# One list sets the order of a hybrid decoder layer: the first half's last projections and the second half's tokens move ahead of pooling and scores

## The chip, the cores and the metric

The kernel runs on one core of a Trainium2 chip. The metric is the device time of one execution in microseconds (us), the median of repeated runs. A profile is one further execution, recorded by the hardware; its span goes from the first instruction to the last.

## What is computed

One layer for 1024 prompt tokens and 8 decode tokens, 1024 channels wide:

```python
p = rmsnorm(x) @ w_in             # 512 pooling + 1792 RWKV columns
u, q = p[..., :512], p[..., 512:]
# A: four groups of 128, trailing windows 2, 4, 8, 16
d = (cs[end] - cs[end - win]) / cnt - u
pool = (d @ pool_w[g]) * pool_scale
# B: RWKV-7, 8 heads of 64
qs = q + (shift(q) - q) * shift_mu
r, k, v, zw, za, zg = split(qs)   # 512, 512, 512, 64, 64, 128
decay = exp(-exp(-softplus(-(w0 + tanh(zw) @ w_lora_up)) - 0.5))
S = S * decay + (S @ aa) * bb + v * k    # token by token
y = S @ r                                # then norm, bonus, gate
x = x + concat(pool, y) @ w_out
x = x + relu(rmsnorm(x) @ w_up)**2 @ w_down
```

## The kernel before

Channels lie on partitions, tokens along the free side. The prompt is cut into four **token blocks** (0 to 255, 256 to 511, 512 to 767, and 768 to 1023 with the 8 decode tokens); blocks 0 and 1 are the first **half**, blocks 2 and 3 the second. Every large fp32 product is made of three passes of a shorter type (`gemm`, L183): tokens are split into `xh` and `xl` and weights into `wh` and `wl`, and each of the eight k-tiles gives three matmuls. So one 128-column tile of the input projection takes 24 matmuls per token block; its result is a tile `pj<m>_<b>` (m the column tile, b the block). Column tiles 0 to 3 are the pooling groups, 4 to 15 the r, k and v of four head pairs, 16 and 17 the low-rank inputs.

The recurrence is done in chunks of 64 tokens. The kernel is written as functions, and one list, `ORDER`, says in which order they are recorded; a scheduler then fixes each engine's queue, with priority by the list, and `tc.high_priority(offset=...)` pulls what stands under it ahead. The letters of the list, with their tiles:

- R0 to R7 (`rkv`): projections of k, r and v of a *unit*, which is a head pair in one half (0 to 3 first half, 4 to 7 second).
- S0 to S7 (`stage1`): the unit's decay and scores. TensorE makes `pw`, `pa`, `pk`, `pb`, `sc` and the transposes `bkt`, `vt`; between them stand chains on VectorE and ScalarE.
- I0 to I7 (`inverse`): the inverse of a triangular matrix, for two units in one token block. It doubles on VectorE, goes once out to memory and back (`inv`, `TX`) and ends in the matmuls `pi`. Its buffers exist once, so one inverse follows another.
- C0 to C7 (`lead_chain`): the state's walk over four chunks (`pcs`, `py`, L588 to L622), always pulled ahead by priority.
- P00, P01, P02 and P10, P11, P12 (`pools`): pooling, first and second half, in three parts. Part 0 has the projections and window sums of groups 0 and 1; part 1 the projections and sums of groups 2 and 3, and the products `po` of groups 0 and 1; part 2 the products `po` of groups 2 and 3. The weight `pw_sb` has one buffer.
- T (`later_tokens`): token blocks 2 and 3. They use the two buffers of `xh` and `xl`, so block 2 can be written only when block 0's last projection has been read, and block 3 after block 1's. The raw tokens lie in the four `wr` buffers that raw weights use too.
- L (`low_rank(1)`): column tiles 16 and 17 of the second half. Q and D are small (rows for the pooling state; the start of the decode tokens).

SyncE's queue issues token loads and the inverse's transfers; GpSimd's issues weights, `pw_sb` and the stores of the mixers' results (`mix`). After the list come the out projection `mx` of the first half, which overlaps C6, I7, C7 and the decode tokens, then that of the second half and the MLP (`up`, `dn`).

Of the kernel before, what the change touches and what calls it, by code (L numbers as in the profile page):

```python
# [16 lines left out]
D = 1024  # L17
NP = 1024
NDEC = 8
T = NP + NDEC  # L20
BLK = [(0, 512), (512, 260), (772, 260)]
SEG = [(0, 256), (256, 256), (512, 256), (768, 264)]
HALF = [(0, 512), (512, 520)]
# [4 lines left out]
LEADX = 300  # L28
# [8 lines left out]
NWH = 6  # L37
NX = 2
QUEUE = 1
ORDER = """R0 S0 R1 S1 P00 I0 Q P01 C0 I1 P02 C1 R2 S2 R3 T S3 L I2 R4 C2 I3 R5 C3 S4 S5 I4 R6 C4 I5 R7 C5 S6 S7 I6 P10 C6 I7 P11 P12 D"""  # L40
NBV = 4
NSEG = 4

# [49 lines left out]
def _build(ctx, nc, tc, I, O, dbg):  # L93
    V, A, PE, SY, GP = nc.vector, nc.scalar, nc.tensor, nc.sync, nc.gpsimd

    def f32(ap):
        return ap.bitcast(F32)
# [49 lines left out]
    def sigm(out, in_, bias, scale, last_bias=0.0):  # L147

        act(out, in_, AF.Exp, bias=bias, scale=scale)
        V.tensor_scalar(out, out, BIG, None, ALU.min)  # L150
        act(out, out, AF.Ln, bias=1.0)
        act(out, out, AF.Exp, scale=-1.0, bias=last_bias)


    def weights(src, into=None):

        out = []
        n = int(np.prod(src.shape[1:]))
        for o in range(0, n, 512):
            w = min(512, n - o)  # L160
            raw = wp.tile([P, 512], F32, tag="wr", name="wr", bufs=NWR)
            if len(src.shape) > 2:
                GP.dma_start(raw.rearrange("p (m c) -> p m c", c=P), src)
            else:
                GP.dma_start(raw[:, :w], src[:, o:o + w])
            if into:
                h, l = into
            else:
                h = wp.tile([P, 512], F32R, tag="wh", name="wh", bufs=NWH)
                l = wp.tile([P, 512], F32R, tag="wl", name="wl", bufs=NWH)  # L170
            with tc.high_priority(offset=LEADW):
                act(h[:, :w], raw[:, :w])
                V.tensor_tensor(l[:, :w], raw[:, :w], f32(h[:, :w]), op=ALU.subtract)  # L173
            out += [(h[:, c:c + P], l[:, c:c + P]) for c in range(0, w, P)]
        return out
# [26 lines left out]
    def token_block(b):  # L202

        c0, n = SEG[b]
        xh = xp.tile([P, KT, 266], F32R, tag="xh", name=f"xh{b}", bufs=NX)
        xl = xp.tile([P, KT, 266], F32R, tag="xl", name=f"xl{b}", bufs=NX)
        rs = xp.tile([P, 266], F32, tag="rs", name=f"rs{b}", bufs=NX)
        X[b] = (xh, xl, rs)
        if b:
            for t, q in zip(X[b][:2], X[b - 1]):  # L210
                act(t[:, :, 0:2], f32(q[:, :, 256:258]))
        acc = big(f"acc{b}", "f" if b % 2 else "e")[:, :512].rearrange("p (k t) -> p k t", k=2)
        raw = []

        def parts(k):
            if b == 0:
                xr = big(f"xr{b}_{k}", ("u0", "u1", "d0", "d1")[k // 2])
            elif b == 1:
                xr = s1.tile([P, 512 if k > 2 else 520], F32, tag=("w", "a", "t", "kk")[k // 2], name=f"xr{b}_{k}")
            else:  # L220
                xr = wp.tile([P, 512], F32, tag="wr", name=f"xr{b}_{k}", bufs=NWR)
            xr = xr[:, :512].rearrange("p (k t) -> p k t", k=2)
            raw.append(xr)
            SY.dma_start(xr, I["xT"][:, k:k + 2, c0:c0 + 256])
            for i in range(2):
                x, g, h = xr[:, i, :], col(V_G1, k + i), xh[:, k + i, 2:258]
                act(h, x, scale=g)
                V.scalar_tensor_tensor(xl[:, k + i, 2:258], x, g, f32(h), ALU.mult, ALU.subtract)

        def square(k):  # L230
            xr = raw[k // 2]
            if k:
                act(xr, xr, AF.Square)
                V.tensor_tensor(acc, acc, xr, op=ALU.add)
            else:
                act(acc, xr, AF.Square)

        for k in range(0, KT, 2):
            parts(k)
            if b > 1:  # L240
                square(k)
            if b == 0 and k == 2:
                yield
        yield
        if b < 2:
            for k in range(0, KT, 2):
                square(k)
        ss = (ps_i if b < 2 else ps_d).tile([P, 512], F32, tag="i" if b < 2 else "d", name=f"ss{b}")
        for i in range(2):
            PE.matmul(ss[:, :256], ON, acc[:, i, :], start=i == 0, stop=i == 1)  # L250
        if b == 3:
            xd, xg = (s1.tile([P, KT, NDEC], F32, tag=x, name=f"xd{x}") for x in ("t", "kk"))
            SY.dma_start(xd, I["xT"][:, :, NP:])
            V.tensor_tensor(xg, xd, vec[:, V_G1:V_G1 + 8].unsqueeze(2).to_broadcast([P, KT, NDEC]), op=ALU.mult)
            act(xh[:, :, 258:266], xg)
            V.tensor_tensor(xl[:, :, 258:266], xg, f32(xh[:, :, 258:266]), op=ALU.subtract)
            V.tensor_tensor(xg, xd, xd, op=ALU.mult)
            V.tensor_reduce(xd[:, 0, :], xg.rearrange("p k b -> p b k"), axis=AX.X, op=ALU.add)
            PE.matmul(ss[:, 256:264], ON, xd[:, 0, :], start=True, stop=True)
        ms, t = (s1.tile([P, 264], F32, tag="pr", name=f"{x}{b}", bufs=3) for x in ("ms", "tt"))  # L260
        with tc.high_priority(offset=LEADX if b > 1 else 0):
            rstd(rs[:, 2:n + 2], ss[:, :n], ms[:, :n], t[:, :n])
            if b:
                act(rs[:, 0:2], X[b - 1][2][:, 256:258])
        yield
# [9 lines left out]

    ahead, late = {}, {}

    def project(m, half, use):
        w = ahead.pop(m, None) or weights(I["w_in"][m])
        for b in (2 * half, 2 * half + 1):  # L280
            if b in late:
                with tc.high_priority(offset=LEADX):
                    next(late.pop(b))
            project_block(m, w, b, use, 0 if b else 2)
# [29 lines left out]
    def low_rank(half):  # L314
        n = HALF[half][1]
        z0 = big(f"z0{half}", "f")
        zw, za = (zp.tile([P, 520], F32R, tag=x, name=f"{x}{half}") for x in ("zw", "za"))
        z1 = zp.tile([P, 520], F32, tag="z1", name=f"z1{half}", bufs=2)
        shifted(12, half, z0)
        shifted(13, half, z1)  # L320
        sigm(z0[0:64, :n], z0[0:64, :n], 0.0, 2.0)
        V.tensor_scalar(z0[0:64, :n], z0[0:64, :n], -2.0, 1.0, ALU.mult, ALU.add)
        for z, r, q in ((zw, R[0], R[1]), (za, R[1], R[0])):
            act(z[r, :n], z0[r, :n])
            V.tensor_tensor(z[q, :n], z0[r, :n], f32(z[r, :n]), op=ALU.subtract)
        sigm(z1[:, :n], z1[:, :n], 0.0, -1.0)
        Zt[half] = (zw, za, z1)
# [491 lines left out]
    def later_tokens():  # L819
        with tc.high_priority(offset=LEADX):  # L820
            late.update((b, token_block(b)) for b in (2, 3))
            next(late[2])
            ahead[16] = weights(I["w_in"][16])
            next(late[3])

    st_d = ExitStack()
    dec = []
# [20 lines left out]
    x1 = []  # L848

    def open_x1(half):  # L850
        c0, n = HALF[half]
        xq = open_pool(ctx, f"x1{half}", side="right", reuse_waits="tile")
        x1.append(xq.tile([P, KT, n], F32, name=f"x1{half}"))
        for k in range(0, KT, 4):
            SY.dma_start(x1[half][:, k:k + 4, :], I["xT"][:, k:k + 4, c0:c0 + n])


    def x1s(m, c, n):

# [23 lines left out]
    open_x1(0)  # L883
    with tc.tile_pool(name="opa", bufs=1, side="right", reuse_waits="tile") as op:
        ops = [mixed(op, k, 0, NMA) for k in range(KT)]
        for m in range(KT):
            out_block(m, weights(I["w_out"][m]), ops, 0, 0, 512)
            next(dec, None)
# [46 lines left out]
    ps_u = open_pool(ctx, "psu", 4, space=PSUM)  # L935
    with tc.tile_pool(name="opb", bufs=1, reuse_waits="tile") as op:
        ops = [mixed(op, k, 1, 3) for k in range(KT - 1)]
        for m in range(KT):
            w = weights(I["w_out"][m, :, :(KT - 1) * P])
            for o in (0, 260):  # L940
                out_block(m, w, ops, 1, o, 260)
        norm2(0, 512, lambda x: op.tile([P, 512], F32, tag="n2", name=x, bufs=2))
        last = [mixed(op, KT - 1, 1, 3)]
        w7 = [w for m in (0, 4) for w in weights(I["w_out"][m:m + 4, :, (KT - 1) * P:].rearrange("m p c -> p m c"))]
        for m in range(KT):
            for o in (0, 260):
                out_block(m, w7[m:m + 1], last, 1, o, 260)
# [4 lines left out]
    w = weights(I["w_up"][0])  # L952
# [20 lines left out]
    for g in range(7):  # L973
        ups_of(4 * g + 4)
        for m in range(KT):
            w = weights(I["w_down"][g, m])
# [7 lines left out]
    ws = [weights(I["w_down"][7, m], None if m < 4 else [x[:, m, :] for x in w7]) for m in range(KT)]  # L984
# [103 lines left out]
```

## Time and profile before

| | before |
|---|---|
| median of 3 runs | 1372.07 us (1369.88 to 1374.78) |
| the profiled execution | 1369.46 us |
| its span | 1367.7 us |
| TensorE busy | 1304.4 us (95%) |
| VectorE busy | 806.9 us (59%) |
| ScalarE busy | 555.2 us (41%) |
| GpSimd busy | 152.2 us (11%) |
| TensorE's mean granted clock | 0.976 |

Busy shares are means over the whole span: the first third holds the input projection and the recurrence, where several engines work, the rest the MLP, where TensorE does. The granted clock is a share of 2.4 GHz. Names such as `L774` are lines of the kernel file of before; in the changed file the lines behind the new function stand 17 lower (L791).

### The profile page before, as it was taken

Reading aid. Unit: us, or ns where it says so; the run is one execution under the profiler, and the core shown is the slowest. Engines: PE = TensorE matmul, PEld = TensorE weight load, DVE = VectorE, ACT = ScalarE, POOL = GpSimd, SP = SyncE. Lnnn points to the kernel's source line nnn. Section 1 sums busy time; section 2 is a strip of 40 time slices with the busy share of each in tenths; the row PEclk is TensorE's granted clock in tenths of the full one; section 3 lists DMA queues with packets and bytes.
Section 4 is the critical chain, followed back from the end, with each engine's and each line's share of the span. In section 5 each row is a group of like instructions: output and inputs, shape, how many; then the busy total and the mean of one; then the engine's idle time right before and its main releaser. Section 6 shows DMA issues by size and latency. Waiting matters only on the chain.

```text
span 1367.7 us, 24214 instructions
## 1 busy us (share of the span) xinstructions
PE 1304.4 (95%) x9748; PEld 1149.8 (84%) x9748; DVE 806.9 (59%) x1782; ACT 555.2 (41%) x1261; POOL 152.2 (11%) x301
## 2 busy tenths in 40 slices
PE   6999996999999899999999999999999999999996
PEld 6988775878877676798999999999999999999986
DVE  7887577747866765748644535445444354453447
ACT  7655766766767667626211212112111121121123
POOL 3112001111100110120010100100000100000000
PEclk9999996999999899999999999999999999999998
DMA  7234123221321542431111111111111111111103
GB/s 226 70 80 115 44 61 74 77 52 54 71 50 42 160 127 79 158 132 60 47 55 39 55 47 40 54 40 47 54 39 55 47 43 50 45 48 48 47 7 124
DMA packets 81647, 94.52 MB, mean 69 GB/s; under 512 B 52504, under 2 KB 58776, under 8 KB 81528
## 3 DMA queue, kind: packets, MB, share of 16 engines
q0 software_dynamic: 20480, 66.04, 15.1%
q1 hardware_dynamic: 59728, 25.10, 7.3%
q8 instruction: 76, 1.25, 0.4%
q10 hardware_dynamic: 1328, 1.85, 0.4%
q14 instruction: 35, 0.29, 0.1%
HBM read 79.67 MB, written 13.51 MB: 68 GB/s over the span
## 4 chain that ended last, share of the span: by engine, by line
PE 77%; ACT 7%; DVE 6%; issue 5%; DMA 3%; POOL 1%; SPq 0%; DVEq 0%; POOLq 0%; ACTq 0%
PE dn L183 26%; PE up L183 26%; PE pj L183 7%; PE mx L183 5%; PE sc L415 2%; PE pcs L599 1%; PE pcs L593 1%; ACT SV L100 1%; DMA cst<-in_consts 1%; ACT TT L100 1%; PE py L589 1%; DVE tm L517 1%; ACT ys L100 1%; PE pcs L588 1%; DVE wl L173 1%
## 5 line engine op out<-in xcount | busy, mean ns | idle before, releaser
L100 ACT ACTIVATE wh<-wr 128x512 fp32r<-128x512 f32 x230 | 143.2, 626 | 357.8 <-PE dn L183 276.2
L183 PE MATMUL up<-h2h,wl 128*128 128x260 f32 (+1 forms) x768 | 245.6, 320 | 0.0
L183 PE MATMUL up<-h2h,wh 128*128 128x260 f32 (+1 forms) x768 | 245.1, 320 | 0.5 <-DVE u L930 0.5
L183 PE MATMUL up<-h2l,wh 128*128 128x260 f32 (+1 forms) x768 | 244.9, 320 | 0.0
L183 PE MATMUL dn<-uh,wl 128*128 128x512 f32 (+1 forms) x720 | 231.0, 321 | 0.0
L183 PE MATMUL dn<-ul,wh 128*128 128x512 f32 (+1 forms) x720 | 230.6, 320 | 0.0
L183 PE MATMUL dn<-uh,wh 128*128 128x512 f32 (+1 forms) x720 | 230.3, 320 | 0.0
L969 DVE TENSOR_TENSOR x<-dn,x 128x260 f32<-128x260 f32 (+1 forms) x192 | 99.1, 516 | 189.6 <-PE dn L183 189.6
L183 PE MATMUL pj<-xh,wh 128*128 128x258 f32 (+3 forms) x576 | 174.8, 303 | 10.8 <-ACT wh L100 9.7
L173 DVE TENSOR_TENSOR wl<-wr,wh 128x512 fp32r<-128x512 f32 x230 | 156.4, 684 | 41.0 <-ACT wh L100 37.6
L183 PE MATMUL pj<-xh,wl 128*128 128x258 f32 (+3 forms) x576 | 172.0, 299 | 0.0
L183 PE MATMUL pj<-xl,wh 128*128 128x258 f32 (+3 forms) x576 | 171.6, 298 | 0.0
L183 PEld LDWEIGHTS up<-h2l,wh 128*128 128x128 f32 x768 | 144.5, 188 | 12.3 <-DVE h2l L912 0.6
L183 PEld LDWEIGHTS up<-h2h,wh 128*128 128x128 f32 x768 | 144.2, 188 | 11.7 <-DVE u L930 0.9
L183 PEld LDWEIGHTS up<-h2h,wl 128*128 128x128 f32 x768 | 144.4, 188 | 11.1
L183 PEld LDWEIGHTS dn<-ul,wh 128*128 128x128 f32 x720 | 135.5, 188 | 10.9 <-issue 0.2
L183 PEld LDWEIGHTS dn<-uh,wh 128*128 128x128 f32 x720 | 135.7, 188 | 10.5
L183 PEld LDWEIGHTS dn<-uh,wl 128*128 128x128 f32 x720 | 135.4, 188 | 10.6 <-issue 0.2
L100 ACT ACTIVATE uh<-u 128x260 fp32r<-128x260 f32 (+1 forms) x96 | 47.2, 492 | 238.6 <-DVE u L931 238.6
L183 PEld LDWEIGHTS pj<-xh,wh 128*128 128x128 f32 x576 | 112.4, 195 | 16.5 <-ACT wh L100 9.7
L930 DVE SCALAR_TENSOR_TENSOR u<-up,rs 128x260 f32<-128x260 f32 (+1 forms) x96 | 49.5, 517 | 120.8 <-PE up L183 114.3
L183 PEld LDWEIGHTS pj<-xl,wh 128*128 128x128 f32 x576 | 112.6, 195 | 3.9 <-issue 2.6
(291 smaller groups left out, 2088.5 us busy)
## 6 DMA issues: line engine op xcount, KB each, us to landing
wr<-in_w_in POOLq DMA_DIRECT2D x72, 256.0 KB, 3.1
wr<-in_w_up POOLq DMA_DIRECT2D x64, 256.0 KB, 2.9
wr<-in_w_down POOLq DMA_DIRECT2D x64, 256.0 KB, 2.9
wr<-in_w_out POOLq DMA_DIRECT2D x26, 256.0 KB, 3.3
xr<-in_xT SPq DMA_DIRECT2D x16, 256.0 KB, 3.7
mr<-mix SPq DMA_DIRECT2D x8, 260.0 KB, 3.5
x<-in_xT SPq DMA_DIRECT2D x2, 1040.0 KB, 7.9
blk<-AA SPq DMA_DIRECT2D x16, 128.0 KB, 2.6
```

The lines of the kernel that those rows point to most:

```text
L100: A.activation(out, in_, func, bias=bias, scale=scale, **k)
L173: V.tensor_tensor(l[:, :w], raw[:, :w], f32(h[:, :w]), op=ALU.subtract)
L183: PE.matmul(ps, lhs, rhs, start=i == 0, stop=i == n - 1)
L415: PE.matmul(scs[h][:, c, :], BK[R[h], c, :, :], AR[R[h], c, :, h, :], start=True, stop=True)
L517: V.tensor_tensor(pr[:, q], l[:, q].unsqueeze(2).to_broadcast([64, m, m, m]), r[:, q].rearrange("p k j -> p j k").unsqueeze(1).to_broadcas ...
L588: PE.matmul(pq[:, u], B.AR[u][:, c, 0, :, :], SV[:, c, u], start=True, stop=True)
L589: PE.matmul(py[u][:, c, :, :], SV[:, c, u], B.AR[u][:, c, 1, :, :], start=True, stop=False)
L593: PE.matmul(pa[:, u], TT[:, 4 * u + c, :, :], Q[:, u], start=True, stop=True)
L599: PE.matmul(pu[:, u], B.BKT[u][:, c, :, :], SV[:, c, u], start=True, stop=True)
L930: V.scalar_tensor_tensor(u, ps[:, :n], 0.0, rs2[:, cs], ALU.max, ALU.mult)
L969: V.tensor_tensor(d, ps[:, :n], d, op=ALU.add)
```

## The change

R2 and R3, the projections of the first half's last two units, move ahead of pooling; all of the first half's pooling follows behind R3, then T. S2 comes behind C1, and low-rank (L) moves ahead of S3. P10 moves from behind S7 to behind C3. The second half's products of tiles 16 and 17 are no longer made tile by tile over blocks 2 and 3, but block by block. Token block 3's `rstd` loses its priority. The loads of the residual input `x1` are recorded behind those of `mixed`.

```diff
-ORDER = """R0 S0 R1 S1 P00 I0 Q P01 C0 I1 P02 C1 R2 S2 R3 T S3 L I2 R4 C2 I3 R5 C3 S4 S5 I4 R6 C4 I5 R7 C5 S6 S7 I6 P10 C6 I7 P11 P12 D"""
+ORDER = """R0 S0 R1 S1 I0 Q R2 C0 I1 R3 P00 P01 P02 T C1 S2 L S3 I2 R4 C2 I3 P10 R5 C3 S4 S5 I4 R6 C4 I5 R7 C5 S6 S7 I6 P11 C6 I7 P12 D"""
...
-        with tc.high_priority(offset=LEADX if b > 1 else 0):
+        with tc.high_priority(offset=LEADX if b == 2 else 0):
             rstd(rs[:, 2:n + 2], ss[:, :n], ms[:, :n], t[:, :n])
...
+    def project_later():
+
+        ws = [ahead.pop(m) for m in (16, 17)]
+        for b in (2, 3):
+            next(late.pop(b))
+            if b == 2:
+                next(late[3])
+            for w, (m, use) in zip(ws, hold):
+                project_block(m, w, b, use, 0)
+
+    hold = []
+
     def project(m, half, use):
+        if m > 15 and half:
+            hold.append((m, use))
+            return
...
         shifted(13, half, z1)
+        if half:
+            project_later()
...
             ahead[16] = weights(I["w_in"][16])
-            next(late[3])
+            ahead[17] = weights(I["w_in"][17])
...
     def open_x1(half):
-        c0, n = HALF[half]
+        n = HALF[half][1]
         xq = open_pool(ctx, f"x1{half}", side="right", reuse_waits="tile")
         x1.append(xq.tile([P, KT, n], F32, name=f"x1{half}"))
+
+    def load_x1(half):
+        c0, n = HALF[half]
         for k in range(0, KT, 4):
...
         ops = [mixed(op, k, 0, NMA) for k in range(KT)]
+        load_x1(0)
...
         ops = [mixed(op, k, 1, 3) for k in range(KT - 1)]
+        load_x1(1)
```

TensorE's queue at the end of the first half's projections, in before: behind R3's last tile (`pj15_1`) come the scores of S3 and the sums of squares of block 2 (`ss2`).

```order
L183 MATMUL pj15_1_2454<-xl1_207,wh_2421 128x258
L183 MATMUL pj15_1_2454<-xh1_206,wl_2422 128x258
L332 MATMUL pw3_0_2569<-zw0_325,wup_127 128x512
L333 MATMUL pw3_0_2569<-zw0_325,lol_129 128x512
L332 MATMUL pa3_0_2580<-za0_326,aup_128 128x512
L333 MATMUL pa3_0_2580<-za0_326,lol_129 128x512
L373 MATMUL pk3_0_2590<-t3_0_2587,cst_86 128x512
L250 MATMUL ss2_2691<-acc2_2488,cst_86 128x256 x2
L183 MATMUL pj16_2_2703<-xh2_2483,wh_2522 128x258
```

The same place in the changed kernel, where the last tile is pooling group 3's:

```order
L183 MATMUL pj3_1_2198<-xh1_206,wl_2143 128x256
L791 MATMUL po1_0_0_2231<-d1_0_1980,pw1_0_2080 128x256
L791 MATMUL po1_0_256_2234<-d1_0_1980,pw1_0_2080 128x256
L791 MATMUL po2_0_0_2257<-d2_0_2089,pw2_0_2238 128x256
L791 MATMUL po2_0_256_2260<-d2_0_2089,pw2_0_2238 128x256
L791 MATMUL po3_0_0_2264<-d3_0_2131,pw3_0_2247 128x256
L791 MATMUL po3_0_256_2267<-d3_0_2131,pw3_0_2247 128x256
L349 MATMUL pw2_0_2440<-zw0_325,wup_127 128x512
L350 MATMUL pw2_0_2440<-zw0_325,lol_129 128x512
L349 MATMUL pa2_0_2451<-za0_326,aup_128 128x512
L350 MATMUL pa2_0_2451<-za0_326,lol_129 128x512
L250 MATMUL ss2_2548<-acc2_2276,cst_86 128x256
```

Three pooling products with their weights, and the scores of S2 (not S3), now stand between the last projection of block 1 and the first of block 2; S3's scores come behind both.

VectorE's queue a little later in the changed kernel: the window sums of pooling group 3 (`d3`, `e3`), then the sums of squares of token block 2 (`acc2`) and the split of a weight.

```order
L776 TENSOR_TENSOR d3_0_2131<-e3_0_2132 128x525
L776 TENSOR_TENSOR e3_0_2132<-d3_0_2131 128x521
L776 TENSOR_TENSOR d3_0_2131<-e3_0_2132 128x513
L784 TENSOR_TENSOR d3_0_2131<-d3_0_2131,cst_86 128x16
L787 SCALAR_TENSOR_TENSOR d3_0_2131<-d3_0_2131,u3_0_2130 128x496
L234 TENSOR_TENSOR acc2_2276<-acc2_2276,xr2_2_2284 128x512
L785 TENSOR_TENSOR d3_0_2131<-d3_0_2131,u3_0_2130 128x16
L234 TENSOR_TENSOR acc2_2276<-acc2_2276,xr2_4_2292 128x512
L234 TENSOR_TENSOR acc2_2276<-acc2_2276,xr2_6_2300 128x512
```

The sums of squares stand behind the window sums, which in before had been done long ahead of them.

GpSimd's queue in before, at the weights of tile 16 of the second half (`wr_2520`, `wr_2526`) and the next two:

```order
L628 DMA mix4_0_78<-ys0_1_1933 128x256
L628 DMA mix5_0_80<-ys0_1_1933 128x256
L165 DMA wr_2520<-in_w_in 128x512
L165 DMA wr_2526<-in_w_in 128x512
L165 DMA wr_2784<-in_w_in 128x512
```

The same in the changed kernel, from the load of pooling group 1's `pw_sb` on (`wr_2308` to `wr_2326` are tiles 16 and 17):

```order
L768 DMA pw1_0_2080<-in_pool_w 128x128
L793 DMA mix0_0_70<-d0_0_1939 128x512
L768 DMA pw2_0_2238<-in_pool_w 128x128
L793 DMA mix1_0_72<-d1_0_1980 128x512
L768 DMA pw3_0_2247<-in_pool_w 128x128
L793 DMA mix2_0_74<-d2_0_2089 128x512
L165 DMA wr_2308<-in_w_in 128x512
L165 DMA wr_2314<-in_w_in 128x512
L165 DMA wr_2320<-in_w_in 128x512
L165 DMA wr_2326<-in_w_in 128x512
```

The loads of tiles 16 and 17 moved behind the store of pooling group 2's result.

TensorE's queue in before, at R7's last tile and the first scores of S6 (`pw2_1`), behind which P10's first tile begins:

```order
L183 MATMUL pj15_3_4850<-xh3_2532,wl_4818 128x266
L332 MATMUL pw2_1_4994<-zw1_2688,wup_127 128x512
L333 MATMUL pw2_1_4994<-zw1_2688,lol_129 128x512
L332 MATMUL pa2_1_5005<-za1_2689,aup_128 128x512
L333 MATMUL pa2_1_5005<-za1_2689,lol_129 128x512
L183 MATMUL pj0_2_5380<-xh2_2483,wh_5370 128x256
```

The same place in the changed kernel, where tile 2 follows at once:

```order
L183 MATMUL pj15_3_5000<-xh3_2560,wl_4968 128x266
L349 MATMUL pw2_1_5144<-zw1_2545,wup_127 128x512
L350 MATMUL pw2_1_5144<-zw1_2545,lol_129 128x512
L349 MATMUL pa2_1_5155<-za1_2546,aup_128 128x512
L350 MATMUL pa2_1_5155<-za1_2546,lol_129 128x512
L183 MATMUL pj2_2_5531<-xh2_2271,wh_5521 128x256
```

The 96 matmuls of `pj0` and `pj1` on blocks 2 and 3 (P10) have moved far ahead, between R4's last tile and R5's first (`pj9_2`); 96, those of `pj2` and `pj3`, stay here.

## Rows read from the trace of the kernel before

**Rows 1.** The page: TensorE's busy time, and its granted clock in 40 slices.
```profile
PE 1304.4 (95%) x9748; PEld 1149.8 (84%) x9748; DVE 806.9 (59%) x1782; ACT 555.2 (41%) x1261; POOL 152.2 (11%) x301
...
PEclk9999996999999899999999999999999999999998
```
**Rows 2.** Windows of the span: stretch, its length, busy time (instructions) per engine, clock, DMA.
```profile
95.70:127.60 31.90, 29.20 (x379) 27.19 (x378) 23.53 (x62) 18.02 (x46) 8.98 (x20) 0.95 0.49 137
186.50:195.30 8.80, 8.80 (x76) 8.80 (x74) 5.03 (x13) 3.84 (x12) 1.61 (x3) 1.00 0.08 30
195.30:231.00 35.70, 21.14 (x83) 15.55 (x81) 29.17 (x67) 22.66 (x52) 4.84 (x9) 0.65 0.42 114
231.00:261.70 30.70, 28.91 (x389) 27.35 (x388) 20.50 (x53) 24.61 (x58) 3.87 (x8) 0.96 0.32 76
261.70:316.00 54.30, 51.66 (x528) 43.77 (x527) 28.07 (x82) 33.03 (x92) 4.97 (x10) 1.00 0.19 52
316.00:376.00 60.00, 58.97 (x420) 52.22 (x419) 53.42 (x130) 40.02 (x91) 7.54 (x14) 1.00 0.24 63
376.00:393.50 17.50, 14.79 (x254) 12.25 (x252) 7.46 (x15) 11.24 (x27) 1.89 (x4) 0.80 0.33 80
393.50:428.50 35.00, 33.04 (x399) 27.43 (x399) 29.40 (x82) 23.56 (x64) 3.35 (x7) 1.00 0.19 50
428.50:466.80 38.30, 34.25 (x212) 27.61 (x210) 30.16 (x84) 25.50 (x62) 4.85 (x9) 0.91 0.31 85
```
**Rows 3.** Timeline of TensorE: start, length, line, tiles; eight landmarks.
```profile
158.90 0.59 PE L593 MATMUL pcs<-Q,TT 128*128 128x128 f32 x3
...
185.07 0.81 PE L622 MATMUL py<-z,glu 128*128 128x256 f32 x3
...
195.29 0.40 PE L332 MATMUL pw<-zw,wup 128*128 128x512 f32 x1
...
230.94 0.57 PE L183 MATMUL pj<-xh,wh 128*128 128x266 f32 x1
...
261.34 0.71 PE L593 MATMUL pcs<-Q,TT 128*128 128x128 f32 x4
...
284.82 0.70 PE L622 MATMUL py<-z,glu 128*128 128x256 f32 x2
...
376.01 0.39 PE L332 MATMUL pw<-zw,wup 128*128 128x512 f32 x1
...
469.72 1.22 PE L183 MATMUL mx<-mh,wh 128*128 128x512 f32 x2 [2.21 <-ACT mh L100]
```
**Rows 4.** Groups of VectorE lines, 113.7 to 125 us: the pooling sums of groups 2 and 3.
```profile
L759 DVE TENSOR_TENSOR d<-e 128x521 f32<-128x521 f32 (+2 forms) x3 | 2.0, 682 | 0.0
...
L759 DVE TENSOR_TENSOR e<-d 128x525 f32<-128x525 f32 (+1 forms) x2 | 1.4, 696 | 0.0
...
L770 DVE SCALAR_TENSOR_TENSOR d<-d,u 128x496 f32<-128x496 f32 x2 | 1.3, 669 | 0.0
...
L298 DVE TENSOR_TENSOR pr<-pj,rs 128x256 f32<-128x256 f32 (+1 forms) x2 | 0.8, 424 | 0.2 <-PE pj L183 0.2
...
L759 DVE TENSOR_TENSOR d<-u 128x527 f32<-128x527 f32 x1 | 0.7, 708 | 4.8 <-DMA mix<-d 4.8
...
L759 DVE TENSOR_TENSOR e<-u 128x527 f32<-128x527 f32 x1 | 0.7, 701 | 0.0
```
**Rows 5.** The group of VectorE lines that splits the tokens, 195.3 to 231 us.
```profile
L228 DVE SCALAR_TENSOR_TENSOR xl<-xr,vec,xh 128x256 fp32r<-128x256 f32 x12 | 5.4, 483 | 2.6 <-ACT xh L100 2.6
```
**Rows 6.** TensorE's waits, 0 to 620 us: total, times, longest.
```profile
PE ss L250 <- DVE acc L234: 4.1, 1, 4.1
...
PE po L774 <- DMA pw<-in_pool_w: 2.0, 1, 2.0
```
**Rows 7.** The page's DMA issues: count, size, median us from issue to landing.
```profile
wr<-in_w_in POOLq DMA_DIRECT2D x72, 256.0 KB, 3.1
...
x<-in_xT SPq DMA_DIRECT2D x2, 1040.0 KB, 7.9
```

## The prediction

> **What bounds the kernel now.** I read the page first, for busy time and clock. TensorE is busy for 1304.4 us of the span, so some 63 us are all that order alone can win; its clock falls in two of the 40 slices ahead of the MLP, the 7th (205 to 239 us) and the 14th (445 to 479 us) [rows 1]. Then the windows, cut at landmarks of the timeline, show what limits each stage [rows 2, 3]. From 95.7 to 195.3 us TensorE is covered: the two inverses and chains of the first half run one after the other, with projections in their gaps, and the last stretch shows a projection matmul's price, 8.80/76 = 0.116 us. From 195.3 to 231.0 us it is bare: 21.1 us of work in 35.7 us at a granted clock of 0.65, so partly at the 1.2 GHz level, while VectorE is busy for 29.2 us (82%). There the token blocks 2 and 3 and S3 are made, and the wait for `acc` (4.1 us) is the visible end of VectorE's queue [rows 6]. From 231 to 376 us TensorE is nearly full again (51.66 of 54.3 us, 58.97 of 60 us). From 376 us to the out projection at 469.7 us chains set the pace once more: C4, I5 and C5 follow each other, with a clock of 0.80 and 0.91 in two of the stretches. Behind 469.7 us the change leaves the work as it is. So the sum asks where two landmarks go: C2's first matmul (261.3 us) and the first `mx` (469.7 us) [rows 3].
>
> **The change part by part.** *Up to the first half's last projection.* R2's projections now come in earlier: by the order 18 more projection matmuls stand ahead of S1's last scores, 18 x 0.116 = 2.1 us, so S1 ends at 97.8 us and not at 95.7. From there two inverses and chains follow serially; in before C1's first matmul comes 158.9 - 95.7 = 63.2 us later [rows 2, 3]. VectorE no longer makes pooling sums in this stretch. Of the 7.8 us of such sums and their inputs (below) perhaps half stood in the path, an estimate, so I take 59.2 us: C1 starts at 157.0 us. The chain itself took 26.2 us beside S2 (158.9 to 185.1) and 23.5 us as C2 (261.3 to 284.8); S2 is gone from there, so 23.5: 180.5 us. Then 40 matmuls of tiles 2 and 3 remain, 4.7 us, and the last projection of block 1 ends at 185.2 us, ten earlier than before. That is no gain yet, since S2 and the pooling products, done by then before, are still to do.
>
> *The stretch behind it.* In before VectorE needs 29.2 us here, with one unit's scores and 12 of the 16 splits of the tokens [rows 2, 5]. Now it has also the window sums of groups 2 and 3: 2.0 + 1.4 + 1.3 + 0.7 + 0.7 us, and four scalings of the projections at 0.424 us, 7.8 us [rows 4]. By the order eight of the 16 splits stand ahead of these, so 4 x 0.483 = 1.9 us fewer remain here. That is 29.2 + 7.8 - 1.9 = 35.1 us; at the same 82% it takes 42.8 us. TensorE cannot fill it: the products of block 2 need `ss2`, which waits for `acc2`, and `acc2` stands behind the window sums on VectorE. What TensorE has ready is `po` and S2's few matmuls. Block 3's first product (230.9 us before) so starts at 185.2 + 42.8 = 228.0 us, but only S2 is done by then; in before S3 was.
>
> The Trainium skill ("TensorE: Matmul & The Clock Gate", Architectural detail) says that ScalarE's and VectorE's queues are strictly first in, first out. By that rule `acc2` cannot overtake the sums, which speaks against the change; the wait of 4.1 us for `acc` in before agrees with it and does not prove it. If `acc2` could pass them, the products of block 2 would come 6.1 us earlier, and the sum would end at 1382.
>
> *S3, R4 and low-rank.* From 316 to 376 us before holds two units' scores with two units' projections: 60 us, VectorE 53.4 us busy [rows 2]. Half is 30 us, and low-rank's own work on VectorE (four more products to shift, scalings, splits of weights) I put at 4.5 us, about ten operations of the sizes just named. S3 ends at 228.0 + 34.5 = 262.5 us. From there to C2's first matmul is one inverse: in before 261.3 - 230.9 = 30.4 us [rows 3]. C2 starts at 292.9 us, 31.6 later than before.
>
> *What is ahead by then.* TensorE has done what in before came behind C2's start: 42 matmuls of R4, the 96 of P10 and 40 of R5, 178 x 0.116 = 20.6 us. From C2 to `pw2_1` before takes 114.7 us and is nearly all TensorE's, so the 82 matmuls of R4 and R5 give back 9.5 us: 105.2 us, and `pw2_1` comes at 398.1 us. From `pw2_1` to `mx` before takes 93.7 us [rows 3] with only 82.1 us of TensorE's work [rows 2]: there the chains C4, I5, C5 set the time, and TensorE waits for them. The 96 matmuls that P10 took away (11.1 us) were their cover, not their cause. Of them I credit 3 us, bounds 0 and 11.1. So `mx` starts at 398.1 + 90.7 = 488.8 us, 19.1 later.
>
> *Queues and small edits.* The loads of tiles 16 and 17 stand behind the store of pooling group 2's result on GpSimd's queue, and need all four `wr` buffers. One such load takes 3.1 us to land [rows 7], and TensorE once waited 2.0 us for `pw_sb` [rows 6]. Three of those weights now follow each other through one buffer, each load behind the `po` before it, with nothing else on TensorE. Bounds are nothing (VectorE's 42.8 us are longer) and 3.1 + 2 x 2.0 = 7.1 us; I take nothing, since VectorE is later there. Doing the low-rank products by block lets block 2's begin before block 3's tokens are split, a gain of at most one block's 24 matmuls, 2.8 us; it stands in a stretch that VectorE sets, so nothing. The `x1` loads and the lost priority of `rstd` I put at nothing: the loads land under the out projection of the half before, and without that cover would cost one landing, 7.9 us [rows 7].
>
> The sum is 1369.5 + 19.1 = 1388.6 us for the profiled execution; I say 1388. The runs' median lies 2.6 us above that execution, which I leave in the range.
>
> **The rivals.** *A, faster: the cover pays in full.* If TensorE is the real bound from C2 on, all 20.6 us come back, and its idle time there shrinks too: from 261.7 to 466.8 us it is busy for 192.7 of 205.1 us, so 12.4 us are the most. C2 to `mx` then takes between 208.4 - 20.6 = 187.8 us and 175.4 us. If VectorE also runs at its full rate in the two stretches (35.1 us, then 31 us) C2 comes at 281.7 us and `mx` between 469.5 and 457.1 us; the middle is 463, 6.4 us earlier: 1363 us. It decides once C2 starts ahead of 290 us with the short stretch, or of 278 with the long one. For it speaks that TensorE's total work is unchanged and its clock would hold at 2.4 GHz; against it the 0.80 and 0.91 granted behind 376 us, where chains set the pace [rows 2].
>
> The Trainium skill ("Perfetto Trace Analysis", Optimization Strategy) advises interleaving regimes whose most-contended engine differs. P10 beside I2 is that, in this rule's favour; pooling, tokens and S2 together put VectorE's work in one place, which is its opposite.
>
> *B, no change.* The two halves cancel: C2 25 us later, and 20.6 + 3 us given back, 1370 us. *C, much slower.* C2 as I say, but nothing of what was pulled ahead pays, since R5's weights or the chains hold the later stages: 292.9 + 208.4 = 501.3 us, 31.6 later, 1401 us.
>
> **How the numbers follow.** The forecast gets 0.46 (with a range of its own of 1376 to 1395), C 0.17, A 0.25, B 0.12. A measurement of this kernel can tell about 0.3% (4 us) from no change. So slower 0.63, same 0.12, faster 0.25. The range, 1362 to 1402, reaches from A's middle to C; half of A and some of C lie outside.
>
> **What would show it.** Right: TensorE largely idle and at the lower level for some 40 us between the last `po` and `pj16_3`, C2's first matmul near 293 us, `pw2_1` near 398, `mx` near 489, and longer chains' waits between these two. VectorE over 80% busy from 185 to 262 us. Wrong: C2 ahead of 280 us (then pooling's sums and S2 overlapped with something that I held serial), or under 82 us from `pw2_1` to `mx` (then the 96 matmuls were a cause after all).

## The result

The changed kernel takes 1381.13 us (median of 7 runs, 1378.34 to 1385.45), the kernel before 1370.37 us beside it (7 runs, 1366.36 to 1374.78): a ratio of 1.0081, 95% interval 1.0055 to 1.0107, so 10.8 us slower. The profiled execution took 1385.27 us with a span of 1383.5 us; it lies at the upper end of its runs, and differs from the profiled execution of before by 15.8 us. So of what the traces show between these two, some 5 us are scatter between executions, not the change.

The page after, TensorE's busy time and its clock:

```profile
PE 1317.4 (95%) x9748; PEld 1159.5 (84%) x9748; DVE 809.3 (58%) x1782; ACT 553.9 (40%) x1261; POOL 152.1 (11%) x301
...
PEclk9999987989988989999999999999999999999999
```

The work is the same (9748 matmuls), but TensorE counts 13.0 us more as busy, and the clock has the two low places of [rows 1] again, each wider: slices 6 and 7 (173 to 242 us) and slices 12 and 13 (380 to 450 us). Two slices more, the 9th and the 15th, show 8 as well.

The landmarks of after on TensorE's timeline (start, length, line, tiles; lines stand 17 lower than in before), beside those of [rows 3]:

```profile
154.58 0.71 PE L610 MATMUL pcs<-Q,TT 128*128 128x128 f32 x4
...
177.29 1.13 PE L639 MATMUL py<-z,glu 128*128 128x256 f32 x4
...
193.83 0.80 PE L349 MATMUL pw<-zw,wup 128*128 128x512 f32 x1
...
227.94 0.78 PE L183 MATMUL pj<-xh,wh 128*128 128x266 f32 x1
...
258.75 0.60 PE L444 MATMUL bkt<-cst,BK 128*128 128x128 f32 x4
...
287.75 0.85 PE L610 MATMUL pcs<-Q,TT 128*128 128x128 f32 x3
...
390.11 0.39 PE L349 MATMUL pw<-zw,wup 128*128 128x512 f32 x1
...
486.29 0.80 PE L183 MATMUL mx<-mh,wh 128*128 128x512 f32 x1 [2.69 <-ACT mh L100]
```

The windows of after that these landmarks cut (as in [rows 2]: length, busy time per engine, granted clock, DMA):

```profile
184.10:227.90 43.80, 30.76 (x120) 21.39 (x119) 36.01 (x79) 26.55 (x60) 8.07 (x15) 0.67 0.31 96
227.90:261.00 33.10, 32.72 (x239) 30.17 (x238) 28.23 (x67) 22.94 (x51) 4.63 (x9) 0.97 0.32 82
287.80:390.10 102.30, 100.33 (x863) 86.89 (x863) 75.62 (x193) 69.05 (x171) 10.47 (x20) 0.98 0.21 55
390.10:486.30 96.20, 79.95 (x767) 61.97 (x765) 60.79 (x163) 59.62 (x154) 8.83 (x18) 0.82 0.23 60
```

| landmark or stretch | before | predicted | after |
|---|---|---|---|
| C1's first matmul | 158.9 | 157.0 | 154.6 |
| last projection of block 1 ends | 195.3 | 185.2 | 184.1 |
| block 3's first product | 230.9 | 228.0 | 227.9 |
| C2's first matmul | 261.3 | 292.9 | 287.8 |
| from there to `pw2_1` | 114.7 | 105.2 | 102.3 |
| from `pw2_1` to `mx` | 93.7 | 90.7 | 96.2 |
| `mx` starts | 469.7 | 488.8 | 486.3 |

The bare stretch is where it was expected, from 184.1 to 227.9 us: VectorE busy for 36.0 of 43.8 us (82%), TensorE's clock 0.67; behind it S3 and R4 run with TensorE full (32.72 of 33.1 us). What ends TensorE's waits there:

```profile
PE po L791 <- DVE d L785: 6.0, 2, 3.3
...
PE pb L401 <- DVE bv L399: 4.4, 1, 4.4
...
PE ss L250 <- DVE acc L234: 0.6, 1, 0.6
```

The three rows add up to 11.0 us: pooling's products wait for the window sums (6.0 us), the scores of S2 for VectorE too (4.4 us), and `ss` for `acc` now only 0.6 us. This `ss` is the one of token block 3, as was the one that waited 4.1 us in before [rows 6]: it comes behind the first products of block 2 (128x258), which start at 203.3 us in before and earlier, at 199.6 us, in the changed kernel.

```profile
203.33 0.78 PE L183 MATMUL pj<-xh,wh 128*128 128x258 f32 x1
...
211.94 1.15 PE L250 MATMUL ss<-acc,cst 128*128 128x256 f32 x4 [4.14 <-DVE acc L234]
```

```profile
199.55 0.47 PE L183 MATMUL pj<-xh,wh 128*128 128x258 f32 x1
```

The window sums act by way of TensorE's queue: behind the pooling products, which wait for them, stand S2's first scores (`pw`, at 193.8 us, 9.7 us behind the last projection) and then block 2's `ss`, which has to wait no more. The next stretches give back less than TensorE did ahead: C2 to `mx` went from 208.4 to 198.5 us, 9.9 us for 20.6 us of work. The last row is the one to look at. The stretch from 390.1 to 486.3 us has 95 matmuls fewer than in before and is 2.5 us longer, at a clock of 0.82 where before had 0.92. The same two stretches in before:

```profile
261.30:376.00 114.70, 110.99 (x946) 96.35 (x947) 81.84 (x211) 73.44 (x182) 12.75 (x25) 1.00 0.21 57
376.00:469.70 93.70, 82.79 (x862) 67.58 (x860) 67.01 (x179) 63.18 (x160) 10.88 (x22) 0.92 0.27 71
```

### The profile page after: what moved, and what is told of

Same layout as the page of the kernel before. It is cut to its first block, busy times and chain, and to the rows that moved or that the text cites. A ratio compares the mean times of both kernels' runs of the same rounds, so it can differ in the third digit from the quotient of the medians.

```text
span 1383.5 us, 24222 instructions
## 1 busy us (share of the span) xinstructions
PE 1317.4 (95%) x9748; PEld 1159.5 (84%) x9748; DVE 809.3 (58%) x1782; ACT 553.9 (40%) x1261; POOL 152.1 (11%) x301
## 4 chain that ended last, share of the span: by engine, by line
PE 82%; ACT 6%; DVE 5%; DMA 3%; issue 2%; SPq 1%; POOL 0%; DVEq 0%; ACTq 0%; POOLq 0%
PE dn L183 26%; PE up L183 26%; PE pj L183 11%; PE mx L183 5%; PE sc L432 3%; PE pcs L610 1%; PE pcs L616 1%; ACT SV L100 1%; ACT ys L100 1%; PE py L606 1%; DMA prevT<-in_state_shiftT 1%; PE py L618 1%; DMA TX<-inv 1%; DMA inv<-Es 1%; PE py L639 1%
## 5 line engine op out<-in xcount | busy, mean ns | idle before, releaser
L183 PE MATMUL pj<-xh,wh 128*128 128x258 f32 (+3 forms) x576 | 176.3, 306 | 12.8 <-ACT wh L100 9.8
L183 PEld LDWEIGHTS dn<-ul,wh 128*128 128x128 f32 x720 | 135.5, 188 | 10.9 <-issue 0.2
L183 PEld LDWEIGHTS pj<-xh,wh 128*128 128x128 f32 x576 | 113.7, 197 | 17.5 <-ACT wh L100 9.8
L183 PEld LDWEIGHTS pj<-xl,wh 128*128 128x128 f32 x576 | 113.7, 197 | 4.2 <-issue 2.9
```

Of the source, the lines that this page charges most:

```text
L183: PE.matmul(ps, lhs, rhs, start=i == 0, stop=i == n - 1)
```

## Experiments

All ratios are to the kernel before on the same chip, with the 95% interval.

**The list alone, and the edits alone.** The kernel before with the new list:

```diff
-ORDER = """R0 S0 R1 S1 P00 I0 Q P01 C0 I1 P02 C1 R2 S2 R3 T S3 L I2 R4 C2 I3 R5 C3 S4 S5 I4 R6 C4 I5 R7 C5 S6 S7 I6 P10 C6 I7 P11 P12 D"""
+ORDER = """R0 S0 R1 S1 I0 Q R2 C0 I1 R3 P00 P01 P02 T C1 S2 L S3 I2 R4 C2 I3 P10 R5 C3 S4 S5 I4 R6 C4 I5 R7 C5 S6 S7 I6 P11 C6 I7 P12 D"""
```

> The kernel before with the new list alone (no block-by-block low-rank products, rstd and x1 as before). Theory (the list is the cause: pooling's sums, tokens and S2 in one stretch bound by VectorE, and P10's early cover not paid back): as slow as the changed kernel, 1377 to 1385 us, with the first product of block 3 near 228 us and C2's first matmul near 288. Rival (the small edits cost it: four weights loaded behind one another, rstd late): back to 1369 to 1374 us.

Measured: 1385.36 us, 1.0115 (1.0092 to 1.0137), just above the expected 1377 to 1385. Block 3's first product comes at 227.3 us as expected, C2 at 295.0, 7 us later than expected. The list is the cause. The changed kernel with the old list:

```diff
-ORDER = """R0 S0 R1 S1 I0 Q R2 C0 I1 R3 P00 P01 P02 T C1 S2 L S3 I2 R4 C2 I3 P10 R5 C3 S4 S5 I4 R6 C4 I5 R7 C5 S6 S7 I6 P11 C6 I7 P12 D"""
+ORDER = """R0 S0 R1 S1 P00 I0 Q P01 C0 I1 P02 C1 R2 S2 R3 T S3 L I2 R4 C2 I3 R5 C3 S4 S5 I4 R6 C4 I5 R7 C5 S6 S7 I6 P10 C6 I7 P11 P12 D"""
```

> The changed kernel with the old list: only the block-by-block products, the earlier weights of tile 17, rstd and the x1 loads. Theory: 1367 to 1373 us, no change against before, since the stretch is VectorE's; at most 2.8 us of gain from block 2's 24 matmuls coming ahead. Rival (the small edits cost it): 1377 us or more.

Measured: 1370.31 us, 1.0000 (0.9985 to 1.0015). With the old list the four small edits are worth nothing. Under the new list they bring C2 from 295.0 to 287.8 us in the traces; in the totals the intervals, 1.0092 to 1.0137 without them and 1.0055 to 1.0107 with them, overlap, so that gain stays unproved. The windows of this kernel from C2 to `pw2_1` and on to `mx`, for the next comparison:

```profile
255.30:373.00 117.70, 114.30 (x973) 99.66 (x972) 83.81 (x214) 74.97 (x185) 13.28 (x25) 1.00 0.21 56
373.00:465.10 92.10, 81.40 (x863) 66.33 (x861) 66.95 (x180) 63.21 (x160) 10.88 (x22) 0.94 0.28 72
```

**P10's place alone.** The old order in the first half, the new one behind it (P11 and P12 move up by a place with it, here and below; they were not tried by themselves):

```diff
-ORDER = """R0 S0 R1 S1 I0 Q R2 C0 I1 R3 P00 P01 P02 T C1 S2 L S3 I2 R4 C2 I3 P10 R5 C3 S4 S5 I4 R6 C4 I5 R7 C5 S6 S7 I6 P11 C6 I7 P12 D"""
+ORDER = """R0 S0 R1 S1 P00 I0 Q P01 C0 I1 P02 C1 R2 S2 R3 T S3 L I2 R4 C2 I3 P10 R5 C3 S4 S5 I4 R6 C4 I5 R7 C5 S6 S7 I6 P11 C6 I7 P12 D"""
```

> The kernel before with P10 (and P11, P12) where the changed kernel has them, and the small edits; the first half's order is the old one. Theory: C2 stays near 261 us, S6's first scores come up to 11.1 us later, and nothing is won from there to the first out product: 1376 to 1382 us, so that P10's place alone is most of the loss. Rival (only the first half's order costs time): 1368 to 1373 us.

Measured: 1378.02 us, 1.0060 (1.0036 to 1.0084). Its two windows, to be held against those just shown:

```profile
257.30:386.40 129.10, 125.64 (x1068) 111.22 (x1068) 91.24 (x231) 78.11 (x193) 15.19 (x29) 1.00 0.22 59
386.40:483.40 97.00, 77.84 (x767) 60.43 (x765) 60.59 (x163) 60.80 (x154) 8.97 (x18) 0.83 0.24 62
```

The first stretch is 11.4 us longer (117.7 to 129.1), which is the price of 96 matmuls, 11.1 us. The second has 96 matmuls fewer and is not shorter but 4.9 us longer (92.1 to 97.0), at 0.83 of the clock and not 0.94. So P10's matmuls had cost nothing where they stood, and cost their full price where they went. Not all of it reaches the end. `mx` comes 18.3 us later than with the edits alone (465.1 to 483.4 us), the first `up` only 11.2 us later (620.6 to 631.8 us), and the median is 7.7 us higher; why the stretch behind `mx` is shorter then wasn't tried. From the first `up` on every one of the eleven traces takes 747.4 to 748.1 us.

**P10 back.** The changed kernel with P10, P11 and P12 where before had them; R5 then comes ahead in P10's place:

```diff
-... I2 R4 C2 I3 P10 R5 C3 S4 S5 I4 R6 C4 I5 R7 C5 S6 S7 I6 P11 C6 I7 P12 D"""
+... I2 R4 C2 I3 R5 C3 S4 S5 I4 R6 C4 I5 R7 C5 S6 S7 I6 P10 C6 I7 P11 P12 D"""
```

> The changed kernel with P10 back behind S7, I6 (and P11, P12 as before); R5 stands beside I2 in its place. Theory (P10 pays nothing back from where it was taken): C2 stays near 288 us, C2 to the first scores of S6 falls from 102 us by up to 11.1 us (96 matmuls) to 91 to 95, and from there to the first out product stays 93 to 96 us: 1372 to 1376 us, some 6 to 11 under the changed kernel. Rival (C2 to S6 isn't TensorE's, or P10's matmuls lengthen the late stretch): 1380 us or more.

Measured: 1367.00 us (12 runs), 0.9985 (0.9964 to 1.0006): the whole loss is gone, more than the theory had it, and both stretches are shorter than expected (87.3 us for 91 to 95, 89.0 us for 93 to 96). C2 starts at 290.1 us, so 28.8 us later than in before, and yet `mx` starts at 466.4, 3.3 us earlier:

```profile
290.10:377.40 87.30, 85.72 (x763) 72.79 (x763) 70.14 (x185) 63.75 (x159) 8.61 (x17) 1.00 0.22 56
377.40:466.40 89.00, 81.60 (x867) 67.11 (x865) 66.56 (x179) 64.01 (x167) 10.05 (x21) 0.96 0.24 64
```

C2 to `mx` takes 176.3 us, where before took 208.4: 32.1 us less for work pulled ahead that I had priced at 20.6 us. With R5 done during I2, S4 begins at C2's start (290.9 us, in before 318.5), and the stretch behind `pw2_1`, with P10 in it, has its clock at 0.96. Behind `mx` the lead is lost again, the first `up` coming at 624.2 us (in before 619.8). This profiled execution, of 1373.52 us, is 6.5 us slower than the median of its kernel, so its landmarks are, if anything, late.

**Work without use in P10's old place.** The changed kernel and, behind I6, 96 matmuls on constant operands whose result nobody reads:

```diff
+    def filler(n):
+
+        for _ in range(n):
+            ps = ps_d.tile([P, 512], F32, tag="d", name="fill")
+            for i in range(24):
+                PE.matmul(ps[:, :256], aup[:, :P], wup[:, :256], start=i == 0, stop=i == 23)
...
-... S6 S7 I6 P11 C6 I7 P12 D"""
+... S6 S7 I6 F4 P11 C6 I7 P12 D"""
```

> The changed kernel with 96 matmuls more, which compute nothing that is used (constant operands, 256 columns), in P10's old place in the list. Theory (P10 was cover there in a second sense: without it TensorE's granted clock falls to 0.82 in the stretch, and every matmul on the chains' path gets slower): the stretch from S6's first scores to the first out product gets shorter with more work in it, 96.2 to 90 to 94 us, at a clock of 0.90 or more: 1375 to 1380 us. Rival (the clock is incidental, the chains on VectorE and ScalarE set the stretch): 96 us or more, 1381 to 1386 us.

Measured: 1379.85 us, 1.0064 (1.0040 to 1.0088). The stretch is shorter, as the theory said:

```profile
286.10:387.50 101.40, 99.31 (x863) 85.53 (x863) 76.19 (x198) 69.05 (x171) 11.01 (x21) 1.00 0.21 56
387.50:480.20 92.70, 84.35 (x867) 69.03 (x865) 60.49 (x164) 61.09 (x157) 8.31 (x17) 0.92 0.25 63
```

92.7 us with 867 matmuls against 96.2 us with 767 in the changed kernel, at a clock of 0.92 and not 0.82. Groups of chain and score matmuls in the stretch, in the changed kernel (mean ns of one behind the busy time, then the idle time ahead of them):

```profile
L432 PE MATMUL sc<-AR,BK 64*128 64x128 f32 x64 | 9.8, 336 | 0.9 <-DVE BK L427 0.9
...
L606 PE MATMUL py<-AR,SV 128*128 128x128 f32 x32 | 7.8, 330 | 1.5 <-DVE SV L622 1.1 <-DVE ys L644 0.3
...
L444 PE MATMUL bkt<-cst,BK 128*128 128x128 f32 x16 | 3.9, 365 | 3.2 <-DVE AR L439 3.2
```

and with the filler:

```profile
L857 PE MATMUL fill<-wup,aup 128*128 128x256 f32 x96 | 18.7, 335 | 0.5 <-issue 0.5
...
L432 PE MATMUL sc<-AR,BK 64*128 64x128 f32 x64 | 8.5, 297 | 0.0
...
L606 PE MATMUL py<-AR,SV 128*128 128x128 f32 x32 | 6.6, 288 | 0.2 <-DVE SV L622 0.2
...
L444 PE MATMUL bkt<-cst,BK 128*128 128x128 f32 x16 | 3.3, 311 | 0.2 <-DVE AR L439 0.2
```

A score matmul takes 297 ns and not 336, one of the chain 288 and not 330 (the chain's other groups fell by 4 to 26 ns), and the waits for `AR` in front of `bkt` shrink from 3.2 to 0.2 us. P10's own matmuls have the same effect: a score matmul takes 292 ns with the edits alone and 372 ns with P10 moved. So the 96 matmuls had been cover in a second sense. In the whole time this is 1.3 us between medians whose intervals overlap: shown in the stretch, by one profiled execution of each, not in the total.

**Which part of the bare stretch binds.** Both kernels have P10 back. One puts the first half's pooling where it was, with S2 still behind C1:

```diff
-ORDER = """R0 S0 R1 S1 I0 Q R2 C0 I1 R3 P00 P01 P02 T C1 S2 L S3 ...
+ORDER = """R0 S0 R1 S1 P00 I0 Q P01 R2 C0 I1 P02 R3 T C1 S2 L S3 ...
```

> The changed kernel with P10 back behind S7 and the first half's pooling where it was before, S2 still behind C1. Theory (VectorE's): 7.8 us of sums leave the bare stretch, at 82% 9.5 us, so block 3's first product comes near 219 us and C2 near 280 us: 1360 to 1366 us. Rival (pooling's sums don't bind, S2 does): C2 stays within 4 us of 290, 1365 to 1370 us.

Measured: 1360.03 us, 0.9918 (0.9897 to 0.9939). Block 3's first product comes at 219.3 us, C2 at 281.6, as expected, and `mx` at 455.0:

```profile
184.20:219.30 35.10, 26.18 (x110) 19.36 (x108) 31.07 (x71) 25.88 (x58) 4.30 (x8) 0.68 0.32 92
...
281.60:369.00 87.40, 85.80 (x764) 72.87 (x763) 70.11 (x185) 63.74 (x159) 8.53 (x17) 1.00 0.23 56
...
369.00:455.00 86.00, 79.93 (x866) 64.84 (x865) 66.57 (x178) 64.01 (x167) 10.06 (x21) 0.99 0.26 66
```

The bare stretch with P10 back and the sums in it, for comparison, and the start of S2's first scores there and here:

```profile
185.10:229.20 44.10, 31.06 (x121) 21.55 (x121) 36.00 (x79) 26.67 (x60) 8.07 (x15) 0.68 0.31 95
...
194.99 0.80 PE L349 MATMUL pw<-zw,wup 128*128 128x512 f32 x1
```

```profile
184.07 0.40 PE L349 MATMUL pw<-zw,wup 128*128 128x512 f32 x1
```

VectorE is busy for 31.1 of 35.1 us (89%) in the bare stretch, 4.9 us less than with the sums in it (36.0 of 44.1 us with P10 back), while the stretch is 9.0 us shorter. So the expected 9.5 us came out, but not by its working (7.8 us of sums, at 82%): the sums cost more than their VectorE time. With them in the stretch the pooling products wait and S2's first scores, queued behind them on TensorE, start 9.8 us behind the last projection; without them they start with its end. The other puts S2 ahead of pooling:

```diff
-ORDER = """R0 S0 R1 S1 I0 Q R2 C0 I1 R3 P00 P01 P02 T C1 S2 L S3 ...
+ORDER = """R0 S0 R1 S1 I0 Q R2 C0 I1 R3 S2 P00 P01 P02 T C1 L S3 ...
```

> The changed kernel with P10 back behind S7 and S2 ahead of pooling, behind R3. Theory (the bare stretch behind block 1's last projection is VectorE's): one unit's scores leave it, about 17 us of VectorE's 36, so block 3's first product comes at 207 to 216 us and not at 228, and C2 at 270 to 278 us; part of it is paid by S2 slowing the chains before: 1355 to 1364 us. Rival (the stretch is set by the token blocks' loads and sums, whatever stands beside them): C2 stays at 286 us or more, 1365 to 1370 us.

Measured: 1360.94 us, 0.9926 (0.9900 to 0.9953). The time is as expected, the reason only half: block 3's first product comes at 220.3 us, not at 207 to 216, and C2 at 282.3, later than the 270 to 278 expected. Its bare stretch, and TensorE's waits there:

```profile
188.50:220.30 31.80, 18.96 (x78) 13.86 (x77) 22.77 (x46) 18.91 (x45) 9.68 (x18) 0.75 0.43 137
```

```profile
PE po L791 <- DMA pw<-in_pool_w: 5.1, 2, 2.6
PE ss L250 <- DVE acc L234: 5.0, 1, 5.0
PE po L791 <- DVE d L785: 2.7, 1, 2.7
```

VectorE, 13 us lighter, is busy for only 72%, so its load alone no longer explains the stretch. These three rows are all of TensorE's idle time there: first the pooling products wait for their weights, which share one buffer, and for a window sum, then block 3's `ss` waits for its sums of squares. Which of them sets the end wasn't tried.

**Tokens first.** The kernel with pooling ahead, and low-rank (so the products of blocks 2 and 3) listed ahead of S2 and S3:

```diff
-... R3 T C1 S2 L S3 I2 R4 C2 I3 R5 C3 S4 S5 ...
+... R3 T C1 L S2 S3 I2 R4 C2 I3 R5 C3 S4 S5 ...
```

> The kernel with pooling ahead and P10 back, and low-rank (so the products of blocks 2 and 3) listed ahead of S2 and S3. Theory (what costs in the bare stretch is that TensorE's next work, the products of blocks 2 and 3, stands behind a unit's scores on VectorE): block 3's first product falls from 219 us to 200 to 208 us, R4 and R5 then cover S2 and S3, C2 comes later (286 to 292 us) with more projections done by then, and the sum of idle time falls: 1348 to 1356 us. Rival (the chain of scores, inverse and C2 sets what follows, whatever covers it): C2 later by 5 to 10 us and 1360 to 1368 us.

Measured: 1359.50 us, 0.9906 (0.9881 to 0.9932). Block 3's first product comes at 206.7 us, C2 at 286.5 and `mx` at 453.7. The bare stretch is short now, with a clock of 0.80:

```profile
184.50:210.00 25.50, 17.38 (x96) 15.68 (x96) 20.75 (x46) 21.87 (x51) 5.39 (x10) 0.80 0.49 145
```

The landmarks are as the theory had them, the time is not (1348 to 1356 us): 12.6 us won in that stretch are 1.3 us at `mx`, and nothing in the total against the kernel with pooling ahead. C2 is 4.9 us later, and C2 to `mx` takes 167.2 us for 173.4. By C7's last `py` (it ends at 549.0 us, there at 545.2) the rest is lost too; why, wasn't tried. Then R4 ahead of S3 as well, and with it R5 ahead of C2:

```diff
-... R3 T C1 S2 L S3 I2 R4 C2 I3 R5 C3 S4 S5 ...
+... R3 T C1 L S2 R4 S3 I2 R5 C2 I3 C3 S4 S5 ...
```

> The same with R4 listed ahead of S3. Theory: the order on TensorE hardly differs up to R4's last tile, so block 3's first product at the same time as with tokens first, S3 a little later, 1348 to 1358 us. Rival (S3's place sets C2): C2 3 us or more later than there and 1360 us or more.

Measured: 1358.42 us, 0.9906 (0.9884 to 0.9928); block 3's first product at 206.8 us, C2 at 291.4. The C2 that the rival asked for came (4.9 us later), its time did not; it is just above the theory's 1348 to 1358 us. All four versions with P10 back and the first half rearranged once more beat both kernels, this one by about 13 us under before, the one with pooling ahead by 11 us; the intervals can't tell them apart.

## Why the prediction came out as it did

The forecast was slower, 1388 us in a range from 1362 to 1402; measured were 1381.1 us. The direction holds, and so do the landmarks up to C2, within 5.1 us; one term failed, and with it the account of where the loss lies. That the sum still ended 2.5 us off at `mx` (486.3 us for 488.8) is luck: C2 came 5.1 us early, 2.9 us more were given back behind it, and P10's place cost 5.5 us more than credited.

- **Up to the last projection of block 1**: 185.2 us forecast, 184.1 found. S1 ends later than I said (its `vt` at 101.0, not 97.8 us), and from there to C1 takes 53.6 us, not 59.2; two errors that partly cancel.
- **The bare stretch**: 42.8 us forecast, 43.8 found, VectorE at the 82% that I took over. That it is VectorE's alone is too simple, as the kernels with pooling ahead and with S2 ahead show. With the sums out of it the stretch loses 9.0 us for 4.9 us of VectorE's work; with S2 out of it VectorE is busy for only 72%, and the waits for pooling's weights, which I had priced at nothing, come to 5.1 us. One reading was wrong: the 4.1 us wait for `acc` in before is block 3's, not block 2's. Block 2's products, which I had held up by `acc2` behind the sums, start 3.8 us earlier than in before, and no wait of their `ss` shows; what shows are the pooling products' waits for the sums, ahead of S2's first scores. Of the signs that I named, VectorE over 80% busy came true (64.2 of 76.9 us from 184.1 to 261 us, 84%); TensorE "largely idle" did not, it was busy for 30.8 of 43.8 us.
- **S3, R4 and the inverse**: C2 came 5.1 us earlier than forecast. Block 3's first product to C2 took 59.9 us, not 64.9. Both halves were shorter: S3's last `bkt` came at 258.8 us, not 262.5, and the inverse then took 29.0 us, not 30.4.
- **The 82 matmuls given back between C2 and `pw2_1`**: 9.5 us forecast, 12.4 found.
- **The step that failed: "Of them I credit 3 us, bounds 0 and 11.1."** Taking P10's 96 matmuls out of the stretch from `pw2_1` to `mx` gave nothing back. The stretch got 2.5 us longer against before, 4.9 us with the first half's order unchanged, which lies outside the bounds. I had held that the matmuls were cover; I had not held that taking cover away lowers the clock under the chains, though 0.80 and 0.91 in [rows 2] stand just where cover is thin. The filler shows it for the stretch, 0.82 to 0.92. That the chains' waits there would get longer, a sign that I did name, is so: TensorE is idle for 16.3 us of it, in before for 10.9.
- **The account**: I laid the loss on C2's start, 31.6 us late, with only part of the 20.6 us repaid. With P10 back C2 is 28.8 us late and the time no worse than before (0.9964 to 1.0006). So the new order of the first half is repaid in full, as rival A said, when what is pulled ahead is R5, on which the next scores wait; it isn't when it is P10, on which nothing waits until the out projection. A's number is met (176.3 us from C2 to `mx`, its lower bound was 175.4), but not for this list, and not by its split: of the 32.1 us less than in before, 26.5 are TensorE's busy time, where A had 20.6, and 5.6 its idle time, where A had up to 12.4. By the two comparisons of P10's place it costs 0.0060 of the time, 8.2 us (edits alone against P10 alone), to 0.0096, 13.2 us (P10 back against the change), which holds all of the 10.8.
- **The small edits** were put at nothing, and measured at 1.0000 with the old list. Under the new list a gain is open.

The sum was made for a profiled execution. That of after took 1385.3 us, 3.3 us under the 1388.6; the median of the runs lies another 4.1 us lower, which makes the 7 us between forecast and median.

## What to carry to other kernels

When work is moved ahead to fill a gap, ask two things of it: does anything on the path wait for it, and was it free where it stood. Here 96 matmuls that had run in the idle time of a chain cost their full price at the new place, 11.4 us, and gave nothing back at the old one. Cover ahead of a late chain was repaid when it was the next chain's own input (R5), not when it was P10; and of several changes in one list, each must be tried alone, since here P10's place hid a first half that, rearranged, is 11 us faster than before.

## What the runs showed of the hardware

A stretch can get shorter with more matmuls in it: 96 of no use took it from 96.2 to 92.7 us, with the mean granted clock up from 0.82 to 0.92 of 2.4 GHz and a score matmul down from 336 to 297 ns. Of the eleven kernels, eight have P10 or the filler in that stretch and a clock of 0.92 to 1.00 there; the three without have 0.81 to 0.83. The Trainium skill ("Perfetto Trace Analysis", Matmul Optimizations) says that the engine scales its power with utilization and wants matmuls back to back; these rows agree as far as the clock shows it.
